# A list scheduler's cost table for TensorE and the DMA queue, one reordered product, and three tiles at other addresses

## The chip, the core and the metric

The kernel runs on one NeuronCore of a Trainium2 chip. The metric is the time of one execution on the device, in microseconds (us), the median of several runs. The engines are TensorE (PE; PEld is its weight load), VectorE (DVE), ScalarE (ACT), GpSimd (POOL) and SyncE (SP), whose queue issues nearly all DMAs.

## The reference

One layer of a decoder trunk over 2048 tokens of width 1024: a gated DeltaNet with 8 heads of 128 beside a cross attention with 4 heads over 256 memory rows, an output projection, a layer norm, a squared-ReLU MLP of width 4096, and a second layer norm.

```python
def gdn_mixer(x, mem_k, mem_v, w_in, conv_w, a_log, dt_bias, gate_norm_w, w_out):
    proj = x @ w_in                          # q, k, v, z (1024 each), a, b (8 each), mq (512)
    qkv = jax.nn.silu(causal_depthwise_conv(qkv, conv_w))
    q = l2_normalize(heads(qkv[..., :GDN_WIDTH]))
    k = l2_normalize(heads(qkv[..., GDN_WIDTH:2 * GDN_WIDTH]))
    v = heads(qkv[..., 2 * GDN_WIDTH:])
    beta = jax.nn.sigmoid(b.astype(jnp.float32))
    g = -jnp.exp(a_log) * jax.nn.softplus(a.astype(jnp.float32) + dt_bias)
    o = chunk_gated_delta_rule(q, k, v, g, beta)
    o = (rms_norm(o, gate_norm_w) * jax.nn.silu(heads(z))).reshape(B, T, GDN_WIDTH)
    m = memory_attention(mq, mem_k, mem_v)
    return jnp.concatenate([o, m], axis=-1) @ w_out

# the layer
mem_kv = layer_norm(mem, mem_ln_g, mem_ln_b) @ w_mem_kv
mix = gdn_mixer(x, mem_k, mem_v, *mixer_params[i])
x = layer_norm(ALPHA * x + mix, ln1_g, ln1_b)
x = layer_norm(ALPHA * x + jnp.square(jax.nn.relu(x @ w_ff1)) @ w_ff2, ln2_g, ln2_b)
```

## The kernel before

**Blocks and stages.** The tokens go through in four blocks of 512. Each block has the projections of the 8 heads (PSUM tiles aq, ak, av, az, and aab for the gates, amq for the memory queries), the DeltaNet in chunks of 128, the memory attention, the output projection (ao), and the MLP (af) in four groups of 1024 of its inner width. Block 0 also makes the memory keys and values (amk, amv) from the normalized memory rows (ym), stores the split input weights in DRAM (wsc), and stores sums of the quadrants of the second MLP weight (tsc); blocks 1 to 3 read these back.

**Three products for one.** A large product is made of three float32r products: each operand is split into a rounded part and the rest. `split` casts on ScalarE (hi) and subtracts on VectorE (lo); `mm3` issues hi by hi, hi by lo and lo by hi. A weight tile lands in wraw (three buffers, 128 x 1024) and is split into whl (four buffers). Thi and Tlo are the split tokens, xh, hq and xl those of the MLP's inner values. The small products of the chunk chain are in full fp32: ptk and ptq transpose k and q, pg and pgt make the cumulated gates and their transpose, pkq is the product of k and q, pc and po are the steps over the chunks with vt, R and the state.

**The MLP's second product.** `ff_seven` uses seven products of quadrants for eight. `SEVEN` lists them as (A operand, B operand, PSUM bank, whether it goes on in that bank, output quadrant): A11·B11, S3, S2, A22, S1, A12·B21, S4. The banks A are tiles of their own; B (A12·B21) and C (S3 and A22) are taken from the two buffers of the tag pb. For an integer B operand the weight is one of the sums in tsc, else a part of w_ff2 itself. `keep_sums`, in block 0 alone, loads quadrants into tiles wq (half of them in the buffers of raw and kq1), subtracts on VectorE and stores them to tsc.

**What sets the order.** No instruction is issued where it is written. A recorder takes each call (so every row of the profile names line 320), `cost` gives it a modelled duration in ns, and `issue` list-schedules them all: an operation can start when its predecessors' modelled ends plus a fixed latency have passed and its tile has a free buffer; each engine takes the ready operation that was recorded first; all DMAs share one modelled channel. The instructions of each engine are then emitted in the order of the modelled starts. On the chip every engine goes through its list in that order and waits on semaphores. For TensorE `cost` sets `load`, the time of loading weights, and `last`, the time until the next product can start; for a DMA, the time on the channel.

Of the kernel before, what the change touches and what calls it, by code (L numbers as in the profile page):

```python
# [8 lines left out]
F32 = mybir.dt.float32  # L9
# [5 lines left out]
P = 128  # L15
TB = 512
# [21 lines left out]
def _prod(v):  # L38
    r = 1
    for a in v:  # L40
        r *= a
    return r
# [92 lines left out]
class Recorder:  # L135
# [47 lines left out]
    @staticmethod  # L183
    def cost(o, name, wr, rd, args, kw):
        e = o.eng
        shapes = [r.shape for r in wr] + [r.shape for r in rd]
        n = max([_prod(s[1:]) for s in shapes] or [1])
        if e == "PE":
            rhs = kw.get("rhs", args[2])
            mo, n = _prod(args[1].shape[1:]), _prod(rhs.shape[1:])  # L190
            f32 = name == "transpose" or isinstance(rhs, Ref) and rhs.buf.dtype == F32
            o.load = 0.8 * mo
            o.last = 2.4 + (0.8334 if f32 else 0.4167) * n
            if name == "transpose":
                return o.last
            if f32:
                return o.last + max(o.last, o.load)
            return o.last
        psum = any(r.buf.psum for r in rd + wr)
        if e == "SP":  # L200
            o.extra = 1700 + _prod(wr[0].shape if wr else rd[0].shape) * 4 / 250.0
            return 450
        scal = [v for v in args[2:] if isinstance(v, Ref)] if name.startswith("tensor_scalar") else []
        scal += [v for k, v in kw.items() if k in ("scalar", "scalar1", "scale", "bias") and not isinstance(v, (int, float))]
        if e == "ACT":
            n = _prod((wr[0]).shape[1:])
            return 52 + 0.833 * n + (0 if psum else 42) + 93 * len(scal) + ((305 if scal else 198) if "accum_out" in kw else 0)
        if e == "DVE":
            fast = not psum and name in ("tensor_copy", "tensor_scalar_mul", "tensor_scalar_add", "tensor_scalar_max",
                                         "memset")  # L210
            return 68 + (0.52 if fast else 1.042) * n + 62 * len(scal) + (7 * n if name == "reciprocal" else 0)
        if name == "memset":
            return 40 + 0.83 * n
        if kw.get("op") == ALU.pow:
            return 300 + 165 * n
        if name == "tensor_copy":
            return 119 + 3.34 * n
        return 150 + 2.1 * n if name == "tensor_tensor" else 176 + 3.34 * n
# [118 lines left out]
def hybrid_layer(  # L337
# [24 lines left out]
    nc = tc.nc  # L362
# [6 lines left out]
    cst = ctx.enter_context(tc.tile_pool(name="cst", bufs=1))  # L369
    wp = ctx.enter_context(tc.tile_pool(name="wp", bufs=1))  # L370
    tp = ctx.enter_context(tc.tile_pool(name="tp", bufs=1))
    pad = ctx.enter_context(tc.tile_pool(name="pad", bufs=1))
    nc.vector.memset(pad.tile([P, 112], F32, name="shift"), 0.0)
    sp = ctx.enter_context(tc.tile_pool(name="sp", bufs=1))
    sm = ctx.enter_context(tc.tile_pool(name="sm", bufs=1))
    ps = ctx.enter_context(tc.tile_pool(name="ps", bufs=1, space=bass.MemoryType.PSUM))
# [53 lines left out]
    rec = Recorder(nc, tc)  # L430
    BN_DIM = nc.vector.BN_STATS_DIM
    nc = rec
# [240 lines left out]
    def dense(b, h, T, G, w0=None):  # L673
        res = {}
        for nm, o in (("q", QO), ("k", KO), ("v", VO), ("z", ZO)):
            w = w0 if w0 and nm == "q" else load_in(b, o // P + h)
            a = bank("a" + nm, "acc")
            project(a, w, T)
            c = slot("c" + nm, "d")
            th = slot("th", "th")  # L680
            if nm == "z":
                nc.scalar.activation(th, a, AF.Tanh, scale=0.5)
                nc.vector.scalar_tensor_tensor(out=c, in0=th, scalar=1.0, in1=a, op0=ALU.add, op1=ALU.mult)
            else:
                gi = o // P + h
                raw = rec.buf(tp, (P, TB + 3), F32, "raw", 2, "raw")
                nc.scalar.copy(out=raw[:, 3:], in_=a)
                nc.gpsimd.tensor_copy(raw[:, 0:3], halo[:, gi].part(gi))
                if b < NB - 1:
                    nc.gpsimd.tensor_copy(halo[:, gi].part(gi), raw[:, TB:TB + 3])  # L690
                nc.scalar.activation(c, a, AF.Copy, scale=cw[:, 72 + gi:73 + gi])
                for j in range(3):
                    nc.vector.scalar_tensor_tensor(out=c, in0=raw[:, j:j + TB], scalar=cw[:, j * 24 + gi:j * 24 + gi + 1],
                                                   in1=c, op0=ALU.mult, op1=ALU.add)
                nc.scalar.activation(th, c, AF.Tanh, scale=0.5)
                nc.vector.scalar_tensor_tensor(out=c, in0=th, scalar=1.0, in1=c, op0=ALU.add, op1=ALU.mult)
            res[nm] = c
            if nm in "qk":
                if "kq" not in res:
                    res["kq"] = [rec.buf(tp, (P, 2, TB), F32R, "kq%d" % u, 1, "kq") for u in range(2)]  # L700
                i = "kq".index(nm)
                split(c, res["kq"][0][:, i].part(i), res["kq"][1][:, i].part(i), KQE)
        par = "ga%d" % (h % 2)
        ss = small("ss", [P, 2 * NC])
        kd = res["kd"] = slot("kd", "s%d" % (h % 2))
        for n, nm in enumerate("kq"):
            pt = bank("pt" + nm, par)
            for c in range(NC):
                nc.tensor.transpose(pt[:, c * P:(c + 1) * P], res[nm][:, c * P:(c + 1) * P], ident)
            for c in range(NC):  # L710
                j = small("j" + nm, [P, P], 1)
                nc.scalar.activation(j, pt[:, c * P:(c + 1) * P], AF.Square,
                                     accum_out=ss[:, n * NC + c:n * NC + c + 1])
            if nm == "k":
                for c in range(NC):
                    nc.scalar.activation(kd[:, c * P:(c + 1) * P], pt[:, c * P:(c + 1) * P], AF.Copy,
                                         scale=G["ekd"][:, h, c:c + 1])
        nc.gpsimd.tensor_scalar_add(ss, ss, 4 * RMS_EPS)
        rk = small("rk", [P, NC])
        nc.gpsimd.tensor_tensor(out=rk, in0=ss[:, :NC], in1=mhalf, op=ALU.pow)  # L720
        res["e4"] = small("e4", [P, NC], 4)
        nc.gpsimd.tensor_scalar_mul(res["e4"], ss[:, NC:], P * RMS_EPS)
        res["vbs"] = small("vbs", [P, NC])
        nc.gpsimd.tensor_tensor(out=res["vbs"], in0=G["betah"][:, h], in1=rk, op=ALU.mult)
        bh = res["bh"] = small("bh", [P, NC])
        nc.gpsimd.tensor_tensor(out=bh, in0=G["beta"][:, h], in1=rk, op=ALU.mult)
        nc.gpsimd.tensor_tensor(out=bh, in0=bh, in1=rk, op=ALU.mult)
        res["nbe"] = small("nbe", [P, NC], 4)
        nc.gpsimd.tensor_tensor(out=res["nbe"], in0=bh, in1=G["neg"][:, h], op=ALU.mult)
        return res  # L730

    def invert(L, par):
# [14 lines left out]
        nc.vector.tensor_copy(Xc, i16.unsqueeze(2).to_broadcast([P, 16, NC]))  # L747
        B = small("Bc", [P, 16, NC], 2)
        for j in range(15):
            w = j + 1  # L750
            nc.vector.stream_shuffle(B[:, :w], Xc[:, :w], [j] * 16 + [16 + j] * 16)
            nc.vector.tensor_tensor(out=B[:, :w], in0=B[:, :w],
# [218 lines left out]
    def keep_sums(u, j):  # L971

        if j == 0:
            B = [t[:, n * TB:(n + 1) * TB].part(n) for t in (tok_tile("wq"), tok_tile("wq")) for n in range(2)]
        else:
            B = [rec.buf(tp, (P, TB + 3), F32, "raw", 2, "wq")[:, :TB] for _ in range(2)]
            kq = rec.buf(tp, (P, 2, TB), F32, "kq1", 1, "wq")
            B += [kq[:, n].part(n) for n in range(2)]
        for n in range(4):
            nc.sync.dma_start(out=B[n], in_=w_ff2[u + 2 * (n // 2), n % 2][:, j * TB:(j + 1) * TB])  # L980
        for i, o, x, y in ((1, 0, 1, 0), (3, 1, 3, 1), (2, 3, 3, 0), (4, 2, 2, 3)):
            nc.vector.tensor_tensor(out=B[o], in0=B[x], in1=B[y], op=ALU.subtract)
            nc.sync.dma_start(out=tsc[u, i][:, j * TB:(j + 1) * TB].part(j), in_=B[o])
# [3 lines left out]
    SEVEN = (("A11", "B11", "A", False, (0, 0)), ("S3", 3, "C", False, (1, 1)), ("S2", 2, "A", True, (1, 0)),  # L987
             ("A22", 4, "C", True, (1, 0)), ("S1", 1, "A", True, (1, 1)), ("A12", "B21", "B", False, (0, 0)),
             ("S4", "B22", "A", True, (0, 1)))

    def ff_seven(b, ff1_tiles, relu2, add, norm2):
        Q = 2 * P
        for g in range(NS):
# [45 lines left out]
            if last:  # L1039
                gb = load_bcast(ln2_g, "l2g"), load_bcast(ln2_b, "l2b")  # L1040
            banks = {}
            for n, (xn, wn, bn, on, (th, nh)) in enumerate(SEVEN):
                if not on:
                    banks[bn] = [bank("af2", ("ga%d" % t) if bn == "A" else "pb") for t in range(2)]
                w = [None, None]
# [223 lines left out]
```

## Time and profile before

| | us |
|---|---|
| median of 3 runs | 2996.72 |
| lowest and highest | 2996.67, 2998.15 |
| the profiled execution | 2999.08 |
| its span, first to last instruction | 2997.4 |
| TensorE busy | 2945.4 (98%) |
| weight loads on TensorE | 2428.1 (81%) |
| VectorE busy | 2168.6 (72%) |
| ScalarE busy | 1520.3 (51%) |
| GpSimd busy | 332.4 (11%) |

The mean granted TensorE clock is 0.995 of full speed. The DMA engines moved 469.85 MB. Busy times are of one profiled execution, and TensorE's products are pipelined, so that its busy time counts overlaps and short gaps alike; the views of waits and of the chain of work that ended last tell more. Line numbers can't tell operations apart here, names of tiles do: af<-Thi,whl is a product into the PSUM tile af with the weights Thi and the moving operand whl, or the other way about.

### The profile page before, as it was taken

The numbers are of one execution on the slowest core, as the hardware profiler recorded it, in microseconds if no ns is written. First come the engines' busy times: TensorE is split into PE (matmuls) and PEld (weight loads), VectorE is DVE, ScalarE is ACT, GpSimd is POOL, SyncE is SP. The second block draws the span as 40 slices with busy tenths as digits, with TensorE's granted clock in tenths as the row PEclk, the third lists the DMA queues.
The fourth block names the chain that finished last, engine by engine and source line by source line (L and its number), as shares of the span: only waits on it lengthen the run. The fifth ranks groups of instructions, "written<-read, shape, count | busy, mean of one in ns | idle before, by whom it ended". The sixth has DMA issues, their size and how long they took to land.

```text
span 2997.4 us, 43880 instructions
## 1 busy us (share of the span) xinstructions
PE 2945.4 (98%) x15300; PEld 2428.1 (81%) x15300; DVE 2168.6 (72%) x5537; ACT 1520.3 (51%) x3582; POOL 332.4 (11%) x808
## 2 busy tenths in 40 slices
PE   7999999999999999999999999999999999999998
PEld 6888788888788878888878887888878888788886
DVE  6898977666777787655577887665667787675667
ACT  5676534544355562544445665344554556444443
POOL 1222100000112211000012221000001222000000
PEclk9999999999999999999999999999999999999999
DMA  6765566656733223444473332244446332324443
GB/s 231 253 218 180 196 209 224 200 183 192 268 142 132 106 89 102 145 137 133 151 268 130 121 119 92 87 152 144 145 159 250 126 134 96 99 88 146 143 147 134
DMA packets 127709, 469.85 MB, mean 157 GB/s; under 512 B 14464, under 2 KB 16896, under 8 KB 109056
## 3 DMA queue, kind: packets, MB, share of 16 engines
q1 hardware_dynamic: 126912, 467.00, 46.2%
q8 instruction: 120, 1.97, 0.3%
q14 instruction: 101, 0.83, 0.1%
q10 hardware_dynamic: 576, 0.06, 0.0%
HBM read 402.97 MB, written 64.03 MB: 156 GB/s over the span
## 4 chain that ended last, share of the span: by engine, by line
PE 88%; DVE 8%; ACT 2%; issue 1%; DMA 1%; POOL 0%; POOLq 0%; ACTq 0%; DVEq 0%; SPq 0%
PE af L320 42%; PE ao L320 8%; PE aq L320 6%; PE ak L320 5%; PE az L320 5%; PE av L320 4%; PE amq L320 3%; PE pc L320 3%; PE pp L320 2%; PE pq L320 2%; PE po L320 2%; PE pkq L320 1%; DVE y L320 1%; PE sps L320 1%; DVE ck L320 1%
## 5 line engine op out<-in xcount | busy, mean ns | idle before, releaser
L320 DVE TENSOR_TENSOR whl<-wraw,whl 128x1024 fp32r<-128x1024 f32 (+1 forms) x446 | 538.7, 1216 | 392.8 <-ACT whl L320 386.1
L320 PE MATMUL af<-Thi,whl 128*128 128x512 f32 (+1 forms) x2304 | 655.9, 369 | 6.9 <-DVE whl L320 4.0
L320 ACT CAST whl<-wraw 128x1024 fp32r<-128x1024 f32 (+1 forms) x446 | 466.1, 1045 | 381.8 <-PE af L320 169.0
L320 PEld LDWEIGHTS af<-Thi,whl 128*128 128x128 f32 x2304 | 421.7, 191 | 78.5 <-DVE whl L320 4.8
L320 PE MATMUL af<-whl,xh 128*128 128x512 f32 x1536 | 476.4, 391 | 3.6 <-DVE whl L320 3.6
L320 PE MATMUL af<-Tlo,whl 128*128 128x512 f32 (+1 forms) x1152 | 424.8, 369 | 0.0
L320 PE MATMUL af<-whl,xl 128*128 128x512 f32 x896 | 347.3, 390 | 0.0
L320 PEld LDWEIGHTS af<-whl,xh 128*128 128x128 f32 x1536 | 288.6, 188 | 68.6 <-DVE whl L320 6.7
L320 PE MATMUL ao<-whl,ch 128*128 128x512 f32 x768 | 249.4, 399 | 0.5 <-DVE y L320 0.5
L320 PEld LDWEIGHTS af<-Tlo,whl 128*128 128x128 f32 x1152 | 220.4, 191 | 34.8
L320 ACT ACTIVATE rl<-af 128x512 f32<-128x512 f32 x128 | 76.5, 598 | 271.0 <-PE af L320 269.0
L320 DVE SCALAR_TENSOR_TENSOR y<-y,af 128x512 f32<-128x512 f32 x224 | 151.3, 684 | 84.1 <-PE af L320 82.9
L320 PEld LDWEIGHTS af<-whl,xl 128*128 128x128 f32 x896 | 168.5, 188 | 35.5
L320 POOL TENSOR_SCALAR ve<-mv 128x1 f32<-128x1 f32 x34 | 23.3, 684 | 1528.8 <-DVE mv L320 1528.8
L320 PE MATMUL aq<-Thi,whl 128*128 128x512 f32 x512 | 181.6, 414 | 7.5 <-ACT Thi L320 7.5
L320 PE MATMUL av<-Thi,whl 128*128 128x512 f32 x512 | 173.0, 402 | 0.0
L320 PE MATMUL ak<-Thi,whl 128*128 128x512 f32 x512 | 172.9, 401 | 0.0
L320 PE MATMUL az<-Thi,whl 128*128 128x512 f32 x512 | 170.2, 400 | 0.0
L320 PEld LDWEIGHTS ao<-whl,ch 128*128 128x128 f32 x768 | 142.6, 188 | 27.0 <-DVE y L320 0.7
L320 PE MATMUL ao<-whl,cl 128*128 128x512 f32 x384 | 153.5, 400 | 0.0
L320 PEld LDWEIGHTS aq<-Thi,whl 128*128 128x128 f32 x512 | 94.3, 192 | 21.5 <-ACT Thi L320 7.5
L320 PEld LDWEIGHTS az<-Thi,whl 128*128 128x128 f32 x512 | 95.9, 190 | 18.8 <-DVE whl L320 0.5
(252 smaller groups left out, 5756.3 us busy)
## 6 DMA issues: line engine op xcount, KB each, us to landing
wraw<-in_w_ff_dram SPq DMA_DIRECT2D x224, 512.0 KB, 4.0
whl<-wsc SPq DMA_DIRECT2D x108, 1024.0 KB, 4.8
wraw<-tsc SPq DMA_DIRECT2D x128, 512.0 KB, 3.3
wsc<-whl SPq DMA_DIRECT2D x36, 1024.0 KB, 4.9
wraw<-in_w_out_dram SPq DMA_DIRECT2D x48, 512.0 KB, 4.1
wraw<-in_w_in_dram SPq DMA_DIRECT2D x35, 512.0 KB, 5.8
wq<-in_w_ff_dram SPq DMA_DIRECT2D x64, 256.0 KB, 4.3
tsc<-wq SPq DMA_DIRECT2D x64, 256.0 KB, 3.3
```

What stands on the lines that cost most here:

```text
L320: o.fn(*[res(a) for a in o.args], **{k: res(v) for k, v in o.kw.items()})
```

## The change

The cost table gets other numbers: a weight load 4 + 0.84 ns per column for 0.8, a float32r product 13.4 + 0.4167 ns per column for 2.4 + 0.4167 (fp32 products and transposes keep theirs), a DMA 330 bytes per ns for 250. The pool pad with one unused tile of 448 bytes per partition and its memset go, and the two buffers of raw get 56 columns (224 bytes) more each: raw's second buffer moves by 224 bytes and the tiles kq0 (which hq shares) and kq1 by 448, and all else stays where it was. And in the first group of block 0 `ff_seven` issues A12·B21 second in place of sixth.

```diff
@@ cost
-            o.load = 0.8 * mo
-            o.last = 2.4 + (0.8334 if f32 else 0.4167) * n
+            o.load = 4 + 0.84 * mo
+            o.last = 2.4 + 0.8334 * n if f32 else 13.4 + 0.4167 * n
...
-            o.extra = 1700 + _prod(wr[0].shape if wr else rd[0].shape) * 4 / 250.0
+            o.extra = 1700 + _prod(wr[0].shape if wr else rd[0].shape) * 4 / 330.0
@@ hybrid_layer
-    pad = ctx.enter_context(tc.tile_pool(name="pad", bufs=1))
-    nc.vector.memset(pad.tile([P, 112], F32, name="shift"), 0.0)
@@ dense
-                raw = rec.buf(tp, (P, TB + 3), F32, "raw", 2, "raw")
-                nc.scalar.copy(out=raw[:, 3:], in_=a)
+                raw = rec.buf(tp, (P, TB + 3 + 56), F32, "raw", 2, "raw")
+                nc.scalar.copy(out=raw[:, 3:TB + 3], in_=a)
@@ keep_sums
-            B = [rec.buf(tp, (P, TB + 3), F32, "raw", 2, "wq")[:, :TB] for _ in range(2)]
+            B = [rec.buf(tp, (P, TB + 3 + 56), F32, "raw", 2, "wq")[:, :TB] for _ in range(2)]
@@ ff_seven
-            for n, (xn, wn, bn, on, (th, nh)) in enumerate(SEVEN):
+            order = [0, 5, 1, 2, 3, 4, 6] if b == 0 and g == 0 else range(7)
+            for n, (xn, wn, bn, on, (th, nh)) in enumerate(SEVEN[i] for i in order):
```

The instructions of TensorE are the same ones in another order, on all engines. Three places follow.

**ScalarE, block 0, around the gates and the first z projection**, before: whl<-wraw is the cast of a weight tile, ck and cv the convolved k and v, jk the squares of k for its norm, pg the cumulated gates.

```order
L320 COPY raw<-av 128x512
L320 ACTIVATE th<-ck 128x512
L320 ACTIVATE cv<-av,cw 128x512
L320 CAST kq<-ck 128x512
L320 ACTIVATE jk,ss<-ptk 128x128
L320 CAST whl<-wraw 128x1024
L320 ACTIVATE jk,ss<-ptk 128x128
L320 CAST abw<-abraw 128x8x16
L320 ACTIVATE el<-pg 128x32
```

The same engine at the same place now:

```order
L320 CAST whl<-wraw 128x1024
L320 CAST abw<-abraw 128x8x16
L320 ACTIVATE th<-ck 128x512
L320 COPY raw<-av 128x512
L320 ACTIVATE cv<-av,cw 128x512
L320 CAST kq<-ck 128x512
L320 CAST whl<-wraw 128x1024
L320 ACTIVATE el<-pg 128x32
```

The cast of the z weights has moved ahead of the work on k and v, and the norms of k (jk) behind; on TensorE 16 products of az now stand ahead of pg, and ptk stands behind all 24 of az, where before ptk and pg came first.

**TensorE, block 1, at the end of the projections of k and v**, before (ak and av are the accumulators of k and v, pgt the transposed gates):

```order
L320 MATMUL ak<-Thi,whl 128x512 x2
L320 MATMUL pg<-gg,triu 128x32
L320 MATMUL pg<-gg,ones 128x32
L320 MATMUL ak<-Tlo,whl 128x512
L320 MATMUL ak<-Thi,whl 128x512
L320 MATMUL pgt<-ident,gc 32x128
L320 MATMUL av<-Thi,whl 128x512
```

And now:

```order
L320 MATMUL av<-Thi,whl 128x512 x2
L320 MATMUL av<-Tlo,whl 128x512
L320 MATMUL pg<-gg,triu 128x32
L320 MATMUL pg<-gg,ones 128x32
L320 MATMUL av<-Thi,whl 128x512 x2
L320 MATMUL av<-Tlo,whl 128x512
L320 MATMUL av<-Thi,whl 128x512 x2
L320 MATMUL av<-Tlo,whl 128x512
L320 MATMUL av<-Thi,whl 128x512 x2
L320 MATMUL pgt<-ident,gc 32x128
```

pg has moved from the end of ak into av, and eight products stand between it and pgt where two stood. In the same stretch ptk moved from the end of av to the end of az.

**SyncE's queue, block 0, where the first sums of w_ff2 are read back** (wq are the quadrants loaded for the sums), before:

```order
L320 DMA wraw<-in_w_ff_dram 128x1024
L320 DMA tsc<-wq 128x512
L320 DMA wraw<-in_w_ff_dram 128x1024
L320 DMA wq<-in_w_ff_dram 128x512 x5
L320 DMA wraw<-in_w_ff_dram 128x1024
L320 DMA wraw<-tsc 128x1024
L320 DMA tsc<-wq 128x512 x2
L320 DMA wq<-in_w_ff_dram 128x512
L320 DMA tsc<-wq 128x512 x4
L320 DMA wraw<-tsc 128x1024
```

And now:

```order
L320 DMA wraw<-in_w_ff_dram 128x1024
L320 DMA wq<-in_w_ff_dram 128x512 x2
L320 DMA wraw<-in_w_ff_dram 128x1024
L320 DMA tsc<-wq 128x512
L320 DMA wraw<-in_w_ff_dram 128x1024
L320 DMA tsc<-wq 128x512 x3
L320 DMA wraw<-tsc 128x1024
L320 DMA wq<-in_w_ff_dram 128x512 x4
L320 DMA wraw<-tsc 128x1024
L320 DMA tsc<-wq 128x512 x4
```

The read of the first sum now comes behind all its stores with one more read of w_ff2 ahead of it.

## Prediction

> **What bounds the kernel now.** I read the page first.
>
> ```profile
> span 2997.4 us, 43880 instructions
> PE 2945.4 (98%) x15300; PEld 2428.1 (81%) x15300; DVE 2168.6 (72%) x5537; ACT 1520.3 (51%) x3582; POOL 332.4 (11%) x808
> PE 88%; DVE 8%; ACT 2%; issue 1%; DMA 1%; POOL 0%; POOLq 0%; ACTq 0%; DVEq 0%; SPq 0%
> ```
>
> TensorE is busy 98% of the span and 88% of the chain is its own. The multiset of its 15300 instructions is the same in both kernels; so only three things can change: its waits, the clock granted to it, and what one instruction costs behind another. The view of its waits says how much there is to win.
>
> ```profile
> PE af L320 <- DVE whl L320: 7.6, 10, 1.5
> PE aq L320 <- ACT Thi L320: 7.5, 1, 7.5
> PE ptk L320 <- DVE ck L320: 5.7, 4, 2.0
> ...
> PE pgt L320 <- DVE gkd L320: 2.9, 3, 1.0
> ...
> PE pc L320 <- ACT vt L320: 1.2, 5, 0.4
> ...
> PE pp L320 <- ACT XB L320: 0.2, 1, 0.2
> ```
>
> The columns are total, times and longest, in us. The view's 21 rows, from 7.6 down to 0.2, add up to 39.2 us; 7.5 of them are the load of the first tokens, which the change does not touch. So 31.7 us, 1.1% of the span, bound any gain from waits, and the question is which rows the new order empties and which it fills.
>
> **The new numbers against the trace.** The chain of waits shows TensorE's true rate in the out projection, alone and mixed with the chunk chain.
>
> ```profile
> 1129.98 0.22 PE pc L320 x2
> 1130.20 0.22 PE po L320 x2
> 1130.43 0.69 PE ao L320 x3
> 1131.12 0.22 PE pc L320 x2
> ...
> 1140.67 29.04 PE ao L320 x128
> ```
>
> 29.04 / 128 = 226.9 ns for one product over 512 columns. The old table said 2.4 + 0.4167 x 512 = 215.7, the new one says 13.4 + 213.4 = 226.8. The multiplications take what they took; only the planner's clock is set right. The Trainium skill, "TensorE: Matmul & The Clock Gate", section "Back-to-back issue gap", gives N/2.4 + 2.5 ns for a warm array, 215.8 ns here; by it the old table would be the right one and the new one 5% long. By that rule TensorE would reach a tile of 24 products 24 x 11 = 0.26 us before the plan expects it, on each of the 14 waits of af for whl 3.7 us in all, an estimate; the trace disagrees with it by 11 ns in every product, and the measurement decides.
>
> What mixing costs: from one pc to the next are 1131.12 - 1129.98 = 1.14 us, and the pieces at their own rates (4 x 0.11 and 3 x 0.2269) make 1.12. A round trip between the two kinds thus costs about 0.015 us. In the new order TensorE leaves a run of float32r products 712 times, before 633 times: 79 x 0.015 = **1.2 us lost**.
>
> **Block 0, from the gates to the memory keys.** The chain, then the windows (TensorE busy, weight loads, VectorE, ScalarE, GpSimd; granted clock; DMA share and GB/s), the waits between 20 and 80 us, and the transfer of the z weights.
>
> ```profile
> 25.72 5.45 PE av L320 x24
> ...
> 32.40 0.60 DVE ck L320
> ...
> 34.48 0.20 DVE gg L320
> ...
> 34.81 1.04 PE pg L320 x4
> 35.85 3.28 PE az L320 x7
> ...
> 39.34 4.41 PE az L320 x17
> ...
> 48.06 1.13 DVE whl L320
> ...
> 49.59 3.03 PE amk L320 x23
> ...
> 55.79 1.05 ACT whl L320
> ...
> 68.36 8.01 PE amv L320 x34
> ```
> ```profile
> 32.00:38.00 6.00, 4.01 (x13) 2.95 (x14) 5.58 (x14) 4.98 (x17) 0.15 (x1) 0.63 0.11 45
> ```
> ```profile
> PE ptk L320 <- DVE ck L320: 2.0, 1, 2.0
> PE amv L320 <- DVE whl L320: 1.2, 1, 1.2
> ...
> PE amk L320 <- ACT whl L320: 1.2, 1, 1.2
> PE pg L320 <- DVE gg L320: 0.8, 1, 0.8
> PE amk L320 <- DVE whl L320: 0.8, 1, 0.8
> ```
> ```profile
> 13.24 0.45 SPq L320 DMA_DIRECT2D wraw<-in_w_in_dram  x1
> ```
> ```profile
> DMA to landing us min/median/max: 11.2/11.2/11.2
> ```
>
> Before, TensorE ends av at 31.17 and waits for the convolution of k, then for the gates; az only begins at 35.85, at a clock of 0.63: 468 ns a product for the first 7 (3.28 / 7), 259 for the other 17. It ends at 43.75. In the new order the z weights, landed at 13.24 + 11.2 = 24.4, are split first: the cast stands ahead of the activations of k and v on ScalarE, and VectorE's subtraction ahead of the last step of ck. Replaying by hand: VectorE comes free near 31.6 (32.40 less an idle 0.8), its whl takes 1.13, so az does two products, waits until about 32.8 (1.2 us), and does 14 more by 32.8 + 14 x 0.227 = 36.0. The gates come 1.13 later than 34.68, at 35.8: no wait, or a short one. pg's 1.04 and 8 more az (1.8) end at 38.8. I take 39.4, with half a us kept back: 4.3 us earlier than 43.75. How much of it lasts? ScalarE now has behind az not only the gated z and the four norms of q, but the norms and scalings of k and two casts (2 x 1.05) that were done before, so the product of k and q begins no sooner than in the old order, near 46; memory keys begin perhaps 1 us sooner than 49.59. What lasts comes behind that: the casts for memory keys 3 and 4 now stand ahead of the copies that wait for TensorE and for a store, which empties the rows of amk and amv (1.2 + 0.8 + 1.2 = 3.2). I take 1 + 3 = **4 us gained**. Bounds: a loss of 1 (the scalings of k ahead of the q norms hold the chunk chain) to a gain of 5 (all that 43.75 - 38.8 shows).
>
> On the clock: the low 0.63 follows gaps of 2.0 and 0.8 us. The Trainium skill, same page, section "HAM oscillation — how this bites in real kernels", says to avoid gaps over about 3.4 us; these two are shorter, though with the slow small products around them the stretch from 31.17 to 35.85 is longer, so this run doesn't settle it. By that rule az would run at full speed after a gap of 1.2. The 0.227 a product that I took for az is the full speed too; the half us kept back stands for less.
>
> **Blocks 1 to 3, gates and keys.**
>
> ```profile
> PE ptk L320 <- DVE ck L320: 3.7, 3, 1.3
> PE pgt L320 <- DVE gkd L320: 2.9, 3, 1.0
> ```
>
> The fence holds two rows of TensorE's waits after 530 us, one of each for each block. With the old, slower modelled DMA the planner thought the z weights late and put the transposes of k before az. Now pg stands behind five or seven av products, pgt behind eight more (8 x 0.227 = 1.8 us behind pg; before, two ak products and the wait made 0.45 + 1.0, so about 1.4 is what its chain needs, and the 0.4 to spare is thin), and ptk behind all 24 of az, 5.4 us later, against a wait of 1.3. The gain is at most 3.7 + 2.9 = 6.6; I take **6.0**. If the z weights are not there, the wait only changes its name: then 2.9 at most.
>
> **The swap.** The waits of TensorE from 505 to 530 us, in block 0's first second-layer group:
>
> ```profile
> PE af L320 <- DVE whl L320: 2.0, 3, 1.5
> ```
>
> The sums of the quadrants of w_ff2 have just been stored there and are read back. A12·B21 needs none of them; placed second, it gives them 24 x 0.227 = 5.4 us more, over three times the longest wait. The transfers change places on the same queue. But A12·B21 and the pair S3, A22 sum in the same two PSUM banks (pb). In the table's order S1's 5.4 us lay between them; now S3 takes the banks straight behind A12·B21, and must wait until VectorE has added each to the output. The first bank is complete six products, 1.36 us, before S3 wants it. An add over 512 columns is about half of whl's 1.13 over 1024, 0.6 by that estimate; behind one such subtraction on VectorE it ends after 1.7, so 0.4 late. 2.0 - 0.4: **1.6 gained**; bounds 2.0 and, with two subtractions ahead of the add in both banks, a loss of 1.
>
> **First layer's start.** At the start of ff1 in each of blocks 1 to 3 (here block 1):
>
> ```profile
> PE af L320 <- DVE whl L320: 1.0, 1, 1.0
> PE af L320 <- ACT whl L320: 0.6, 1, 0.6
> ```
>
> Three blocks of 1.6 and, in block 0, a like pair: about 7 us. The chain there (transpose, Thi, Tlo, cast, subtraction) is VectorE's, and the new order only slides a few products in front. **1.5 gained**, 0 to 4.
>
> **The address move.** Of the first-layer products only those that read hq change their offset.
>
> ```profile
> L320 PE MATMUL af<-whl,xh 128*128 128x512 f32 x1536 | 476.4, 391 | 3.6 <-DVE whl L320 3.6
> ...
> L320 PE MATMUL af<-whl,hq 128*128 128x512 f32 x256 | 80.1, 394 | 0.0
> ```
>
> 256 x 3 ns = **0.8 gained** if the offset is the cause, nothing if not. Removing the pad takes one small set instruction before the first load lands: nothing.
>
> **What the truth takes away.** The old 11 ns too few per product meant that TensorE came to each handoff late by 33 ns per three products of filler. That cover goes. Of the chunk chain's handoffs (8 heads x 16 chunks x 3, for vt, R and state: 384) only a few waited before: 1.2 us in 5 for vt, 0.24 each. I put **3 us lost** for a dozen more; bounds 0 and, at 60 waits, 14. The weights' modelled 3.29 us for 512 KB against
>
> ```profile
> wraw<-in_w_ff_dram SPq DMA_DIRECT2D x224, 512.0 KB, 4.0
> ```
>
> is 0.7 short (the old 3.80 was 0.2 short): a late issue costs 0.7 where no tile is waiting ahead. With three raw and four split tiles I put nothing; five such places would cost 3.5.
>
> **The sum.** -4 - 6.0 - 1.6 - 1.5 - 0.8 + 1.2 + 3 = -9.7 us. The profiled run took 2999.08 with a span of 2997.4: 1.7 outside the span, unchanged. It stands 2.4 above the median 2996.72 of three; on the median's scale 2996.7 - 9.7 = **2987.0**. A measurement here tells about 0.2%, 6 us, from no change: faster is below 2990.7, slower above 3002.7.
>
> **Rivals.** *The gains stay, but the waits move* (0.18). The gates' 4 us are given back to ScalarE's longer queue, ff1 gives nothing, and the thin 0.4 of pgt fails half of the time: 0 - 4.5 - 1.6 - 0.8 + 1.2 + 3 = -2.7, so 2994. For it: the product of k and q waits for ScalarE before as after. Against it: the casts for the memory weights do come forward. *The chunk chain loses its cover: slower* (0.13). The fillers between vt, R and state are two to four products. If one handoff in four of the 384 waits 0.24 us, that is 96 x 0.24 = 23.0 us in place of my 3: -9.7 - 3 + 23.0 = +10.3, so 3007.0. It decides from (12.7 + 6) / 0.24 = 78 waits on, one handoff in five. For it: the cover of 33 ns per three products does go. Against it: only 5 of 128 waited for vt before, at that cover. *Late weights* (0.02): if 330 GB/s makes the plan use 20 of the 224 tiles of w_ff 0.7 us early, +14 - 9.7 = +4.3, so 3001. *The table hardly matters* (0.01): then only the swap and the addresses are left, -1.6 - 0.8 = -2.4, so 2994; the rows of the order differ by thousands, so that is nearly out.
>
> **The numbers.** The forecast, 2987.0, has 0.66. Its own bounds: all gains at their best, -5 - 6.6 - 2 - 4 - 0.8 + 1.2 = -17.2, so 2979.5; gains at poorer values (1 at the gates, 4.5 in blocks 1 to 3, 0.8 for the swap, nothing for the rest) with 1.2 and 5 lost, -0.1, so 2996.6. The range takes in the moved waits and the lower end of the slower cases, and a little below the best sum for waits that I have not priced: 2978 to 3001; outside are most of the chunk chain (0.11) and 0.05 below. Faster: 0.60 of the forecast's 0.66, which has only its poorer ends above 2990.7, and 0.05 of the moved waits: 0.65. Slower: the chunk chain, and half of the late weights: 0.14. No change: the other 0.21.
>
> **What will show it.** In the new profile the rows ptk<-ck and pgt<-gkd should be nearly gone from TensorE's waits; az in block 0 should end near 39.4, memory values near 72 in place of 76.4; the whl row between 505 and 530 us should fall below 0.4; TensorE's total of waits from 39 to some 28. The forecast is wrong if the rows of pc (1.2 and less) grow past 15 in sum, if az in block 0 runs at a low clock all the same, or if rows of whl appear in the steady stretches of the second layer, where there are none now.

## The result: slower by half a per cent

The changed kernel took 3011.62 us (median of 6 runs, 3009.34 to 3018.75) against 2997.2 us of the kernel before on the same chip (6 runs, 2996.23 to 2999.29): a ratio of 1.0052, 95% interval 1.0039 to 1.0065, or 14.4 us more. The forecast was 2987.0, in a range of 2978 to 3001. The profiled run took 3010.92 us with a span of 3009.2. Its page, the lines that answer to those of before:

```profile
span 3009.2 us, 43876 instructions
PE 2954.4 (98%) x15300; PEld 2417.7 (80%) x15300; DVE 2175.5 (72%) x5536; ACT 1522.7 (51%) x3582; POOL 320.1 (11%) x808
PE 80%; DVE 8%; ACT 5%; DMA 4%; POOL 1%; issue 1%; SPq 0%; POOLq 0%; DVEq 0%; ACTq 0%
```

TensorE's share of the chain fell from 88% to 80%; ScalarE rose from 2% to 5% and the DMAs from 1% to 4%. TensorE's waits (total, times, longest):

```profile
PE af L320 <- DVE whl L320: 11.0, 11, 3.0
PE aq L320 <- ACT Thi L320: 7.2, 1, 7.2
PE pp L320 <- ACT Q L320: 5.8, 10, 0.9
PE pkq L320 <- ACT jq L320: 2.9, 2, 2.7
PE sps L320 <- ACT pr L320: 2.5, 5, 0.6
PE ptq L320 <- ACT kd L320: 2.3, 2, 2.0
PE pt L320 <- DVE y L320: 1.9, 2, 1.7
...
PE pc L320 <- ACT vt L320: 0.8, 2, 0.4
PE pc L320 <- DVE R L320: 0.6, 1, 0.6
...
PE pc L320 <- DVE state L320: 0.3, 1, 0.3
```

The rows ptk<-ck (5.7 us) and pgt<-gkd (2.9) are gone, as forecast. In their place stand other small steps: pp for Q (inside the inversion of each chunk's triangular matrix), sps for pr (the memory attention), ptq for kd. The chunk and memory attention rows together (pp, pq, pc, sps, pmT, pmo, pto, ptq) have grown from 5.3 us to 14.4. The whole view, 39.2 us before and forecast to fall to some 28, adds up to 41.3. So the sum of the listed waits does not account for the 14.4 us.

Where the time went is told by the starts of TensorE's 15300 products, cut where the same stage ends in each trace (us; the last two columns belong to experiments below, rounding leaves up to 0.2):

| stage | before | changed | changed, old TensorE numbers | changed, MARGIN 96 |
|---|---|---|---|---|
| to the end of the memory values | 76.0 | -6.2 | -4.1 | -4.6 |
| heads, chunks, out projection, block 0 | 369.0 | +11.9 | -0.2 | +1.8 |
| the same, blocks 1 to 3 | 1107.3 | +14.4 | +2.7 | +3.7 |
| MLP without its last 116 af products | 1235.1 | -10.6 | -7.7 | -14.6 |
| those 116 of each block, and from there to the end of the next block's first z projection | 197.8 | +2.5 | -8.6 | -11.4 |
| all, to the last product | 2985.2 | +12.0 | -17.9 | -25.1 |
| of that, lost at half the clock (an estimate, see the last section) | 9.8 | +6.2 | -1.8 | -7.3 |

The fifth row is kept as one stretch, because in it the end of the MLP is mixed with the next block's first projections, and the kernels mix them differently. Before, 24 aq products of the next block lie ahead of the MLP's last product, in the changed kernel 17, with MARGIN 96 only 11. At the usual time of each product, the end of the MLP holds about 11 us more delay in the changed kernel than before, and the stretch from there to the end of the first z projection about 8 us less.

So the gains came and were larger than forecast: 6.2 us at the start, about 8 at the gates and keys of blocks 1 to 3, and 10.6 in the MLP. They were lost again, and 12 more, in the stretches where TensorE trades small products with ScalarE and VectorE (+26.3), and at the ends of the blocks (about 11). About half of the 12 us went where TensorE ran at half its clock.

### The profile page after: what moved, and what is told of

Read it like the earlier page. It is cut to its first block, busy times and chain, and to the rows that moved or that the text cites. A ratio compares the mean times of both kernels' runs of the same rounds, so it can differ in the third digit from the quotient of the medians.

```text
span 3009.2 us, 43876 instructions
## 1 busy us (share of the span) xinstructions
PE 2954.4 (98%) x15300; PEld 2417.7 (80%) x15300; DVE 2175.5 (72%) x5536; ACT 1522.7 (51%) x3582; POOL 320.1 (11%) x808
## 4 chain that ended last, share of the span: by engine, by line
PE 80%; DVE 8%; ACT 5%; DMA 4%; POOL 1%; issue 1%; SPq 0%; POOLq 0%; DVEq 0%; ACTq 0%
PE af L320 40%; PE av L320 5%; PE ao L320 5%; PE ak L320 5%; PE az L320 5%; PE aq L320 4%; PE pc L320 3%; DVE y L320 2%; PE pp L320 2%; PE pq L320 2%; PE amq L320 2%; PE po L320 2%; PE pkq L320 1%; DVE whl L320 1%; PE pmo L320 1%
## 5 line engine op out<-in xcount | busy, mean ns | idle before, releaser
L320 PE MATMUL av<-Thi,whl 128*128 128x512 f32 x512 | 183.3, 409 | 0.0
L320 DVE SCALAR_TENSOR_TENSOR y<-y,af 128x512 f32<-128x512 f32 x224 | 147.1, 683 | 12.9 <-PE af L320 12.8
L320 POOL MEMSET Y<- 128x512 f32 x32 | 16.8, 526 | 1096.9 <-PE af L320 927.6
```

The source lines that it names most:

```text
L320: o.fn(*[res(a) for a in o.args], **{k: res(v) for k, v in o.kw.items()})
```

## Experiments

All times are medians in us, each beside runs of the kernel before on the same chip (2996.7 to 2998.4); ratios are with their 95% intervals.

### One part at a time

The four parts of the diff, each alone on the kernel before.

```diff
# pe_only
+            o.load = 4 + 0.84 * mo
+            o.last = 2.4 + 0.8334 * n if f32 else 13.4 + 0.4167 * n
# dma_only
+            o.extra = 1700 + _prod(wr[0].shape if wr else rd[0].shape) * 4 / 330.0
# swap_only
+            order = [0, 5, 1, 2, 3, 4, 6] if b == 0 and g == 0 else range(7)
# addr_only: the pad out, raw 56 columns longer
```

TensorE's numbers alone. 

> Only the two TensorE numbers of the table are new. Theory A (the true product time takes away the cover that the chunk chain lived on): most of the loss is here, about 3006 to 3012 us, with the new waits of pp, sps and pc in the projections of each block (some 15 us more than before). Theory B (the faster modelled DMA brings weight loads, casts and subtractions ahead of the chain's small steps on ScalarE and VectorE): about no change, 2993 to 3000 us, because the order of the weight traffic stays.

The DMA rate alone. 

> Only the modelled DMA rate is new, 330 for 250. Theory A: no loss, and the gain where the transposes of k and the gates waited in blocks 1 to 3 (6 to 8 us): 2988 to 2993 us. Theory B: the loss is here, 3005 to 3012 us, with late weights at the end of a block and ScalarE in the chain.

The reordered product alone. 

> Only A12 x B21 second in block 0's first group. Both theories: the three waits for whl between 505 and 530 us go, 2 to 2.6 us gained, 2994 to 2995 us; if the order behind it shifts and costs elsewhere, 2996 to 3000.

The addresses alone. 

> Only the pad goes and raw gets longer, so that raw's second buffer, kq0 with hq, and kq1 move. Both theories: products with hq as weights fall from 394 to 391 ns each, 0.8 us, and TensorE's small excess in the steady stretches of the second layer (0.5 us a group) to 0.3: 1 to 3 us gained, 2994 to 2996. If the offset is not the cause: 2997 within 1.

| | median | ratio |
|---|---|---|
| pe_only | 3016.05 | 1.0063 (1.005 to 1.0075) |
| dma_only | 2984.62 | 0.9954 (0.9941 to 0.9966) |
| swap_only | 2998.6 | 1.0 (0.9992 to 1.0009) |
| addr_only | 2997.79 | 1.0 (0.9991 to 1.0009) |

TensorE's numbers cost 18.8 us, the DMA rate gains 12.7, the other two can't be told from nothing. Theory B falls: the faster modelled DMA is a gain. Theory A named the right part; but the waits of pe_only are not all where it put them:

```profile
PE af L320 <- DVE whl L320: 11.3, 12, 3.0
...
PE pg L320 <- DVE gg L320: 6.1, 3, 2.2
PE pgt L320 <- DVE gkd L320: 4.6, 3, 1.5
PE ptk L320 <- DVE ck L320: 2.5, 1, 2.5
PE pp L320 <- ACT Q L320: 2.3, 6, 0.5
...
PE sps L320 <- ACT pr L320: 1.8, 3, 0.6
```

Here the gates of blocks 1 to 3 are waited for longer than before (pg and pgt, 10.7 us against 2.9), since nothing moves them behind av; the chunk stages of blocks 1 to 3 with the out projection lose 12.7. In the changed kernel the DMA rate mends the gates and the chunks' loss stays.

The reordered product's own wait did not go:

```profile
PE af L320 <- DVE whl L320: 2.9, 2, 1.4
```

That is swap_only from 505 to 532 us, against 2.0 in three before. In dma_only, without the reordering, TensorE has no wait for whl in that stretch, and this first group of the second layer, 41.6 us before, is 3.3 us shorter, as in the changed kernel (3.4, with no wait for whl there either). The address move does what it can: hq as weights, in addr_only,

```profile
L320 PE MATMUL af<-whl,hq 128*128 128x512 f32 x256 | 78.9, 389 | 0.0
```

against 394 ns before, and the steady groups of the MLP are each 0.1 to 0.3 us shorter; a total of about 2 us lies under what the comparison can tell.

### TensorE's numbers taken back, and each of the two alone

```diff
# no_pe: the changed kernel with
+            o.load = 0.8 * mo
+            o.last = 2.4 + (0.8334 if f32 else 0.4167) * n
# last_only: only o.load goes back;  load_only: only o.last goes back
```

> The changed kernel with TensorE's two old numbers: new DMA rate, reordered product and addresses stay. If the parts simply add (DMA rate -12.7, the other two 0): 2982 to 2986 us. If the 14.4 us lost come from a clash of the reordered product or the addresses with the new rate, it stays over 2992.

> As the changed kernel, but the modelled weight load stays at 0.8 ns a column; only the product time is new (226.8 ns for 512 columns). Theory A1: the whole loss is here, 3008 to 3014 us. If the longer load of 111 ns (it sets the small fp32 products' pace in the model) is the cause: 2982 to 2990.

> As the changed kernel, but the modelled product stays at 215.7 ns; only the weight load is new (4 + 0.84 ns a column). Theory A1: like the kernel without any of TensorE's new numbers, 2982 to 2988 us. If the load is the cause: 3006 to 3014.

| | median | ratio |
|---|---|---|
| no_pe | 2981.42 | 0.9948 (0.9936 to 0.996) |
| load_only | 2985.52 | 0.996 (0.9946 to 0.9974) |
| last_only | 3000.78 | 1.001 (1.0002 to 1.0019) |
| the changed kernel | 3011.62 | 1.0052 (1.0039 to 1.0065) |

Without TensorE's new numbers the change is a gain of 16.3 us: the two numbers cost 30.2 here, though only 18.8 on the kernel before, so the parts of the change do not simply add. The product time is most of the 30.2 (19.4 alone). The load's 4.1 alone, and the 6.7 that come only with both, are hardly more than the 5 us that a mere reordering is worth below. The expectation that the whole loss lies in the product time is not borne out. In no_pe the waits of the small steps are nearly those of before (5.6 us):

```profile
PE af L320 <- DVE whl L320: 5.0, 6, 1.2
...
PE pp L320 <- DVE X L320: 0.7, 2, 0.4
PE pc L320 <- DVE R L320: 0.5, 2, 0.3
```

### A loss of allowance, or a bad draw?

The order of thousands of instructions hangs on the table; any other number gives another order. First, changes that mean nothing but another order: 0.4 ns in the constant of the product time, in the changed kernel (13.4) and in no_pe (2.4).

```diff
# k130, k138: the changed kernel with
+            o.last = 2.4 + 0.8334 * n if f32 else 13.0 + 0.4167 * n     # k138: 13.8
# no_pe_k20, no_pe_k28: no_pe with
+            o.last = 2.4 + 0.8334 * n if f32 else 2.0 + 0.4167 * n      # no_pe_k28: 2.8
```

> The changed kernel with 13.0 in place of 13.4 ns in the product's time: 0.4 ns of 227, which means nothing for the chip or for any cover, but gives another order. Theory A1 (lost cover, a systematic loss): 3009 to 3014 us, as the changed kernel. Theory A2 (the exact order is a draw): off by 5 us or more in either way, from 2990 to 3015.

> The same with 13.8, 0.4 ns the other way. Theory A1: 3009 to 3014 us. Theory A2: 2990 to 3015, not the same as at 13.0 nor at 13.4.

> The changed kernel with TensorE's old numbers but 2.0 in place of 2.4. Theory A1: as with 2.4, 2980 to 2984 us. Theory A2: spread of the same size as around 13.4, so 2978 to 2998. If both hold (a level set by the cover, and a draw around it): within 6 us of 2981, and clear of the values around 13.4.

> The same with 2.8. Theory A1: 2980 to 2984 us. Theory A2: 2978 to 2998. Both: within 6 us of 2981.

| constant | 2.0 | 2.4 | 2.8 | 13.0 | 13.4 | 13.8 |
|---|---|---|---|---|---|---|
| median | 2981.83 | 2981.42 | 2977.06 | 3006.3 | 3011.62 | 3009.27 |
| ratio | 0.9944 | 0.9948 | 0.993 | 1.0026 | 1.0052 | 1.0034 |

Both theories hold, at different sizes: a draw is worth some 5 us, as far as three draws a group can tell, and between the two groups lie at least 24. (The load differs between the groups too.)

Second, more and less allowance. `issue` adds MARGIN to each latency between engines; 33 ns is what three products of 11 ns took away.

```diff
# margin (63), m46, m96, m140: the changed kernel with
-MARGIN = 30
+MARGIN = 63
# k24: the changed kernel with 24.0 for 13.4
# margin_old (63), m96_old: no_pe with a larger MARGIN
```

> The changed kernel with the scheduler's MARGIN, added to each latency between engines, at 63 ns in place of 30: the 33 ns that three products of 11 ns used to hide. Theory A1 (the loss is the lost cover, and any allowance gives it back): 2983 to 2992 us, the waits of pp, sps and pc back under 4 us together. Theory A2 (every new set of numbers gives another order, and this one is a bad draw; what is lost has to do with where whole stages fall, not with the size of a handoff): anywhere, and no nearer to 2985 than to 3012, say 2995 to 3015.

> The changed kernel with 24.0 in place of 13.4: the model takes 237 ns for a product that takes 227, so TensorE comes to each handoff earlier than planned. Theory A1: worse than the changed kernel, 3015 to 3035 us. Theory A2: like any other draw, 2995 to 3012.

> The changed kernel with MARGIN 46, half of the added 33 ns. Theory A1: between 30 and 63, 2992 to 3004 us. Theory A2: anywhere from 2982 to 3014.

> The changed kernel with MARGIN 96. Theory A1: the waits of the chunk chain go on falling, but each chain is planned longer; 2978 to 2990 us. Theory A2: anywhere from 2982 to 3014.

> TensorE's old numbers, the other parts of the change, and MARGIN 63. Theory A1: the allowance was there already, so at most a few us better and perhaps worse than with 30: 2977 to 2988 us. If MARGIN is worth 26 us by itself and has nothing to do with the product time: 2952 to 2960.

> The changed kernel with MARGIN 140. Theory A1 with a limit: the curve 3012, 2997, 2985, 2975 at 30, 46, 63, 96 flattens; 2970 to 2978 us, few waits of the chunk chain left. If too long a modelled chain sends TensorE past work that is ready: 2980 to 2995.

> TensorE's old numbers, the other parts of the change, MARGIN 96. It has about the allowance of the true numbers with 130: 2969 to 2977 us, as with 63 or a little better; over 2980 if the limit is passed.

The last two columns: what the chunk stages with the out projection take against before in the traces (us, all four blocks), and the median over all runs of the mean granted clock.

| | product of 512 in the model, ns | MARGIN, ns | median | ratio | chunk stages | clock |
|---|---|---|---|---|---|---|
| k24 | 237 | 30 | 3046.61 | 1.0157 (1.0144 to 1.017) | +51.9 | 0.9905 |
| changed | 227 | 30 | 3011.62 | 1.0052 (1.0039 to 1.0065) | +26.3 | 0.992 |
| m46 | 227 | 46 | 2997.39 | 1.0 (0.9991 to 1.0009) | +22.8 | 0.993 |
| margin | 227 | 63 | 2985.37 | 0.9958 (0.9946 to 0.9971) | +10.8 | 0.997 |
| m96 | 227 | 96 | 2975.03 | 0.9928 (0.9915 to 0.9941) | +5.5 | 0.998 |
| m140 | 227 | 140 | 2978.46 | 0.9937 (0.9924 to 0.9949) | +12.8 | 0.996 |
| no_pe | 216 | 30 | 2981.42 | 0.9948 (0.9936 to 0.996) | +2.5 | 0.996 |
| margin_old | 216 | 63 | 2973.89 | 0.9919 (0.9907 to 0.9932) | +1.1 | 0.997 |
| m96_old | 216 | 96 | 2991.8 | 0.9982 (0.9973 to 0.9991) | +11.0 | 0.993 |

From 237 ns down, each step of allowance gains, 35.0, 14.2, 12.0 and 10.3 us, and in the same order the chunk stages lose less. Four steps in one direction, each at least twice a draw, are hard to put down to draws. Nor is MARGIN a gain by itself: the same 33 ns more gain 26.3 us with the true product time and 7.5 with the old one, which held allowance already. So the loss follows the allowance. Beyond the best value the two kinds of allowance part. With the true product time 96 and 140 ns differ by less than a draw; with the old one 96 ns is 17.9 us slower than 63. If 11 ns a product were worth 33 ns of MARGIN throughout, m96_old should be like a kernel with some 129 ns, and m140 beside it is 13.3 us faster; why is not known. Of the expectations k24's loss and the gains of m96 and margin_old were larger than said, m96_old fell outside, and with MARGIN 63 the rows of pp, sps and pc came to 5.6 us in place of under 4.

m96 and margin_old, level within a draw, are the fastest kernels of the study, 22 to 23 us under the kernel before. In m96 the small steps wait little, 7.4 us in all, though the true product time is in the table:

```profile
span 2972.1 us, 43892 instructions
PE af L320 <- DVE whl L320: 4.3, 4, 1.1
...
PE pp L320 <- ACT XB L320: 1.5, 6, 0.3
...
PE pp L320 <- ACT Q L320: 1.0, 5, 0.3
...
PE pc L320 <- DVE R L320: 0.3, 1, 0.3
```

and in k24 they wait most:

```profile
PE af L320 <- DVE whl L320: 13.0, 11, 3.0
...
PE pp L320 <- ACT Q L320: 5.7, 12, 1.0
PE pt L320 <- DVE y L320: 4.7, 7, 2.5
...
PE sps L320 <- ACT pr L320: 3.2, 3, 1.1
```

MARGIN does not undo the change everywhere: in block 0's chunk stage the kernel with 63 is still 7.1 us slower than before (the changed kernel 11.9). At the ends of the blocks it does: the delay of about 11 us there is gone with 46 ns and more.

## Why the prediction was wrong

**The step that failed** is "What the truth takes away": 3 us for a dozen waits, at most 14. With the rest of the change in place the two numbers cost 30.2 us, alone 18.8. That the cover goes was named rightly, there and in the second rival (0.13), and that rival's 3007.0 came within 5 us of the measured time. But both counted the cover at the handoffs of vt, R and the state, and there it hardly mattered: the rows of pc came to 1.7 us against 1.5 before, far from the 15 that were to show the forecast wrong. So the rival had the cause, and its size in part by luck. The runs showed three things in place of the 3 us:

- Other handoffs. The rows of pp for Q, sps for pr, ptq for kd and pt for y grew from 1.6 us to 12.5. The forecast had counted the waits of before and not looked at these.
- The ends of the blocks, put at nothing (below).
- The clock. The prediction names it as one of three things that can change, and gives it no term in the sum beyond half a us kept back at the z projection. Half the clock cost an estimated 6 us more than before.

A count of gaps shows the first and the third in the chunk stages. Take the gap between the starts of two successive products of TensorE, and compare it with the median, over both traces, of the gaps with the same three tiles (of the two products and of the one ahead of them). Gaps over 60 ns too long were 55 before, 11.2 us too long in all. In the changed kernel 94 of them, 24.3 us, lie outside the half clock, and 40 more, 6.7 us, inside it.

A list schedule places each step as close to its predecessors' modelled end as it can, so a smaller modelled lead takes allowance from many handoffs at once. Why Q, pr and kd then wait, and vt, R and the state do not, no run explains. The chain into one wait shows what can happen, block 0, changed kernel:

```profile
319.16 0.60 ACT th L320
...
319.78 0.29 ACT XB L320
...
320.10 0.28 ACT jk L320
...
320.39 0.20 ACT jk L320
320.59 0.26 ACT kd L320
320.85 0.11 ACT Q L320
...
321.00 1.08 PE pp L320 x7
```

Q, 0.11 us on this chain, for which TensorE stands still, is behind a tanh and norms of other work on ScalarE; TensorE waited 0.9 us.

**The ends of the blocks** had been put at nothing. The stretch of the MLP's last 116 products of block 0 is 5.0 us longer in the changed kernel and that of block 2 2.8, though both hold fewer products of the next block; the wait at 795.15 us, 2.0 us long, is the one at block 0's end:

```profile
774.55 7.63 DMA wraw<-in_w_ff_dram
...
790.70 0.52 issue
791.22 0.16 DVE y L320
791.38 0.50 issue
791.88 1.94 DVE y L320 x3
793.82 0.14 DVE gab L320
793.96 1.14 DVE whl L320
795.10 0.04 issue
795.15 2.27 PE af L320 x6
```

The weight was cast in time; VectorE ran the layer norm's steps and the next block's gates before its subtraction. From 795.9 us on the clock was at half for 3.4 us. The modelled 3.29 us for a transfer, against 7.63 here among others, may have its part, but dma_only has only 1.7 us there; this points to the order on VectorE.

**Block 0's start: right in kind, larger in size.** The first z projection ended at 36.6 (forecast 39.4, before 43.75). The product of k and q waited for ScalarE, 2.7 us, as the forecast said, but began at 43.71 and not near 46; the memory keys began at 47.06 for 49.59, without a wait from there to the end of the values at 70.15 (forecast 72, before 76.37). That is 6.2 us for the forecast 4, over its bound of 5.

```profile
34.66 1.94 PE az L320 x8
43.71 1.65 PE pkq L320 x6
47.06 12.18 PE amk L320 x96
59.24 10.91 PE amv L320 x48
```

**Blocks 1 to 3, gates and keys: right.** The two rows are gone, and corrected for the moved products the stretch is about 8 us shorter for the forecast 6.0. It is about 8 in dma_only and no_pe too, so the DMA rate makes this gain and TensorE's new numbers, which lose 10 there on the kernel before, take nothing from it here.

**The swap: wrong in size and cause.** The group is 3.4 us shorter for the forecast 1.6, which had a bound of 2.0. The DMA rate alone does it, and the swap alone does not (2.9 us of waits remain). **First layer's start:** 5.0 us gained in blocks 1 to 3 and 1.3 lost in block 0, for 1.5. Most of it is luck with the clock: the waits there fell only from 1.6 to 1.3 us a block, but behind those of before the clock was at half for 3.4 us in each of the three blocks, and in the changed kernel in none. swap_only has the waits of before in blocks 2 and 3 without the half clock and is 1.5 us faster in each. **Addresses:** right. Where the tiles have moved, the usual product with hq takes 389 or 390 ns, in the changed kernel too; where they have not, 394 to 396. These products belong to the second layer, not the first. **Mixing:** 1.14 us less 1.12 is 0.02 and not 0.015, so 1.6 us by the prediction's own rows. no_pe has 701 round trips, nearly the 712 of the changed kernel, and is 30.2 us faster, so this was never the point.

## What to carry to other kernels

A scheduler's cost table is not only a description; an error that makes the bound engine too fast in the model can be an allowance at its handoffs, and a correction takes it away at many of them at once. When such a number is made true, give the allowance back where it belongs, as a margin on the latencies, and sweep it: here 30 to 96 ns moved the time by 36.6 us, more than the change as a whole. Before believing any single order, change a number by nothing (0.4 ns) twice: that spread, 5 us here, is the size under which a gain is a draw. And read the granted clock beside the waits: here about half of the loss lay in stretches at half the clock.

## What the runs showed of the hardware

**The granted clock fell to half where TensorE had hardly stopped.** In the changed kernel, TensorE alone in the 3.4 us before the fall, and behind it (busy; clock; DMA share and GB/s):

```profile
318.10:321.50 3.40, 2.50 (x21) 1.00 0.99 304
321.50:331.70 10.20, 10.20 (x45) 0.50 0.37 127
```

The only listed wait was 0.9 us, yet the clock was at half for 10.2 us of busy TensorE, which is about 5.1 us lost. The prediction cited the Trainium skill's rule of gaps over some 3.4 us ("TensorE: Matmul & The Clock Gate", section "HAM oscillation — how this bites in real kernels"); this stretch had no such gap. In the kernel before, too, the half clock of block 0 began at 33.5 us, behind the wait of 2.0 us alone. In k24 it came with no listed wait at all, among small products:

```profile
2423.90:2427.30 3.40, 3.24 (x27) 0.99 0.00 0
2427.30:2430.70 3.40, 3.40 (x16) 0.50 0.00 0
```

The same waits do not always bring it: in block 2 the first layer's start has waits of 1.0 and 0.6 us both in the kernel before and in swap_only, and the clock fell only in the first (0.51 against 1.00 from 1924.5 to 1928.0 us). What sets the threshold is left open.

**What it cost.** Up to the last product the clock was at half in stretches of 3.4, 6.8 or 10.2 us: 20.5 us in the kernel before, 34.1 in the changed one, 6.8 with MARGIN 96. Half of TensorE's busy time in them is the estimate of the table: 9.8, 16.0 and 2.5 us. That is one execution of each kernel. Over all runs the median of the mean granted clock is 0.992 for the changed kernel, and 0.996 for the kernel before in the runs beside the experiments. This difference of 0.004 is 12 us of 3010, an upper bound, since a low clock during a wait costs nothing. The clock also goes with the spread between executions of one kernel: of the 12 of m46 the fastest, 2988.86 us, has 0.996, and the three slowest, 3001.77 to 3003.58, have 0.991.
